# A batched two-layer MLP on one core: the framework's frame closed early, and results 4 to 7 on SyncE's ring

## The chip, the cores and the metric

The kernel runs on one core of one Trainium2 chip. The metric is the device time of one execution in microseconds (us). A profile of one execution comes with it; its span runs from the first to the last instruction of the program, and the execution's own time is a little longer than its span.

The core has five engines with a program each: PE (TensorE, matrix products), ACT (ScalarE), DVE (VectorE), POOL (GpSimd) and SP (SyncE, which here only waits and issues transfers). They meet through semaphores. Transfers go through 16 DMA engines that all queues share.

## What is computed

For each of 8 experts, 256 rows of `x` go through two matrices with a ReLU between them:

```python
n_experts, capacity, hidden, expert_hidden = 8, 256, 512, 2048
h = np.matmul(x, w1)          # x: [8, 256, 512]   w1: [8, 512, 2048]
h = np.maximum(h, 0)
return np.matmul(h, w2)       # w2: [8, 2048, 512]
```

All are float32 in memory: 4 MB of `x`, 32 MB of each weight, 4 MB of results.

## The kernel before

**Tiles and stages.** `w1` and `w2` of an expert are one transfer each (L96, L100; 4 MB read, 2 MB written, since the transfer casts to bfloat16). There are two buffers for each, so experts alternate; the last `w2` comes in two pieces (L103, L104). `x` comes in two halves of four experts: `x_f`, float32, issued by SP (L82), and `x_c`, cast by the transfer, issued by POOL (L106). ACT and DVE copy each half to `x_b`; PE transposes it (L203) to PSUM; DVE and ACT take it out to `xt` (L147, L145); DVE cuts an expert's part of it to `xe` (L151). For each expert PE then runs the first product (L215, 64 matmuls in four groups; ACT and DVE apply the ReLU to alternate groups, L167 and L185), then the second (L232, 32 matmuls), whose two halves DVE and ACT copy to the result buffer `o_sb` (L189, L169), which holds all 8 experts.

**Order.** Nothing is scheduled by a planner: the whole kernel is one critical section (L59) inside the frame that the Tile framework opens in `kernel` (L269), and each engine's order is written out. PE runs loops of its own, two turns for the transposes (L198) and four of two experts each (L206), and takes tokens from semaphores at L193. The loops over experts on the other engines are unrolled.

- SP issues `x_f` (L82), then waits in turn for each expert's weights and gives PE a token for each (L84 to L89). Then it waits for the last expert's result (L90, L91), issues it (L92, result 7), and at the end waits for all three transfers of results (L243).
- POOL issues `x_c`, then the weights of experts 0 and 1, with the identity matrix in between (L109, L111); each later load waits until PE has read the buffer (L123, L125). Behind the last load it issues results 0 to 5 as one transfer (L129) and, when expert 6 is done, result 6 (L132).

Transfers that one engine issues go through that engine's ring in order: POOL's is queue q0 in the profile, SP's is q1; q8 carries instructions.

**The frame.** Where the section begins, each engine branches into it (L269) on a semaphore that SP raises. Where it ends (L59), SP waits for every engine's drain; then the frame's end (L269) has each engine drain, meet the others, has POOL clear a range of semaphores, and has the engines meet once more. `no_gpsimd_drain=True` leaves POOL's drain out of the section's end, not out of the frame's.

Of the kernel before, what the change touches and what calls it, by code (L numbers as in the profile page):

```python
# [9 lines left out]
def kernel(  # L10
# [7 lines left out]
    nc = tc.nc  # L18
    P = 128
    bf = mybir.dt.bfloat16  # L20
    f32 = mybir.dt.float32
    relu = mybir.ActivationFunctionType.Relu

    E, C, H = x.shape
    F = w1.shape[2]
    MT = C // P
    KT1 = H // P
    KT2 = F // P
# [10 lines left out]
    def x_rows(g):  # L39
        return x[g * G:(g + 1) * G].rearrange("e c k -> (e c) k").rearrange(  # L40
            "(p j) k -> p j k", p=P
        )
# [13 lines left out]
    po = [nc.alloc_psum_tensor(f"pt_o{m}", [P, H], f32) for m in range(MT)]  # L56
    pt = [nc.alloc_psum_tensor(f"pt_tr{b}", [P, J, P], bf) for b in range(2)]

    with tc.tile_critical(no_gpsimd_drain=True):  # L59
        sem = nc.alloc_semaphore  # L60
        s_x = [sem(f"s_x{g}") for g in range(2)]
        s_w1 = [sem(f"s_w1_{e}") for e in range(E)]
        s_w2 = [sem(f"s_w2_{e}") for e in range(E)]
        s_w2b = sem("s_w2b")
        s_out = [sem(f"s_out{i}") for i in range(3)]
        s_id = sem("s_id")
        s_act = sem("s_act")
        s_dve = sem("s_dve")
        s_tr = sem("s_tr")
        s_h = sem("s_h")  # L70
        s_o = sem("s_o")
        t_xb = sem("t_xb")
        t_pt = [sem(f"t_pt{b}") for b in range(2)]
        t_xe = sem("t_xe")
        t_w = sem("t_w")
        t_ha = sem("t_ha")
        t_hb = sem("t_hb")

        sp, pool, act, dve, pe = nc.sync, nc.gpsimd, nc.scalar, nc.vector, nc.tensor


        sp.dma_start(x_f[:], x_rows(0)).then_inc(s_x[0], 16)  # L82
        for e in range(E):
            sp.wait_ge(s_w1[e], 16).then_inc(t_w, 1)  # L84
            if e < E - 1:
                sp.wait_ge(s_w2[e], 16).then_inc(t_w, 2)
            else:
                sp.wait_ge(s_w2[e], 16).then_inc(t_w, 1)
                sp.wait_ge(s_w2b, 16).then_inc(t_w, 1)  # L89
        sp.wait_ge(s_act, E)  # L90
        sp.wait_ge(s_dve, E)  # L91
        sp.dma_start(out_r[:, E - 1], o_sb[:, E - 1]).then_inc(s_out[2], 16)  # L92


        def load_w1(e):
            pool.dma_start(w1_sb[e % 2][:], w1_r[e]).then_inc(s_w1[e], 16)  # L96

        def load_w2(e):
            if e < E - 1:
                pool.dma_start(w2_sb[e % 2][:], w2_r[e]).then_inc(s_w2[e], 16)  # L100
            else:
                b = w2_sb[e % 2]
                pool.dma_start(b[:, :CUT], w2_r[e, :, :CUT]).then_inc(s_w2[e], 16)  # L103
                pool.dma_start(b[:, CUT:], w2_r[e, :, CUT:]).then_inc(s_w2b, 16)  # L104

        pool.dma_start(x_c[:], x_rows(1)).then_inc(s_x[1], 16)  # L106
        load_w1(0)
        load_w2(0)
        pool.memset(identity[:], 0.0).then_inc(s_id, 1)  # L109
        pool.wait_ge(s_id, 1)  # L110
        pool.affine_select(  # L111
            out=identity[:],
            in_=identity[:],
            compare_op=mybir.AluOpType.not_equal,
            fill=1.0,
            base=0,
            pattern=[[-1, P]],
            channel_multiplier=1,
        ).then_inc(s_id, 1)
        load_w1(1)  # L120
        load_w2(1)
        for e in range(2, E):
            pool.wait_ge(s_h, NQ * (e - 1))  # L123
            load_w1(e)
            pool.wait_ge(s_o, MT * (e - 1))  # L125
            load_w2(e)
        pool.wait_ge(s_act, E - 2)
        pool.wait_ge(s_dve, E - 2)
        pool.dma_start(out_r[:, :E - 2], o_sb[:, :E - 2]).then_inc(s_out[0], 16)  # L129
        pool.wait_ge(s_act, E - 1)  # L130
        pool.wait_ge(s_dve, E - 1)
        pool.dma_start(out_r[:, E - 2], o_sb[:, E - 2]).then_inc(s_out[1], 16)  # L132


        def take_x(g, half):

            for k in range(KT1):
                if k % 2 != half:
                    continue
                eng = act if half else dve  # L140
                eng.wait_ge(s_tr, g * KT1 + k + 1)
                src = pt[k % 2][:].rearrange("p (l m) q -> p l m q", m=MT)
                dst = xt[g][:, k].rearrange("p m (q l) -> p l m q", l=G)
                if half:
                    act.copy(dst, src).then_inc(t_pt[1], 1)  # L145
                else:
                    dve.tensor_copy(dst, src).then_inc(t_pt[0], 1)  # L147

        def give_xe(e):
            g, i0 = e // G, (e % G) * P  # L150
            dve.tensor_copy(xe[e % 2][:], xt[g][:, :, :, i0:i0 + P]).then_inc(t_xe, 1)  # L151


        HALF = J // 2
        act.wait_ge(s_x[0], 16)
        act.copy(x_b[:, :HALF], x_f[:, :HALF]).then_inc(t_xb, 1)  # L156
        take_x(0, 1)
        act.wait_ge(s_x[1], 16)
        act.wait_ge(s_tr, KT1)
        act.copy(x_b[:, :HALF], x_c[:, :HALF]).then_inc(t_xb, 1)  # L160
        take_x(1, 1)
        s_xt = sem("s_xt")
        act.drain().then_inc(s_xt, 1)  # L163
        for e in range(E):
            for q in range(0, NQ, 2):
                act.wait_ge(s_h, NQ * e + q + 1)
                act.activation(ht[e % 2][:, FB * q:FB * (q + 1), :], ph[0][:], relu).then_inc(t_ha, 1)  # L167
            act.wait_ge(s_o, MT * e + 2)
            act.copy(o_sb[:, e, 1, :], po[1][:]).then_inc(s_act, 1)  # L169


        dve.wait_ge(s_x[0], 16)
        dve.tensor_copy(x_b[:, HALF:], x_f[:, HALF:]).then_inc(t_xb, 1)  # L173
        take_x(0, 0)
        dve.wait_ge(s_x[1], 16)
        dve.wait_ge(s_tr, KT1)
        dve.tensor_copy(x_b[:, HALF:], x_c[:, HALF:]).then_inc(t_xb, 1)
        take_x(1, 0)
        dve.wait_ge(s_xt, 1)
        give_xe(0)  # L180
        give_xe(1)
        for e in range(E):
            for q in range(1, NQ, 2):
                dve.wait_ge(s_h, NQ * e + q + 1)
                dve.tensor_relu(ht[e % 2][:, FB * q:FB * (q + 1), :], ph[1][:]).then_inc(t_hb, 1)  # L185
            if e + 2 < E:
                give_xe(e + 2)
            dve.wait_ge(s_o, MT * e + 1)
            dve.tensor_copy(o_sb[:, e, 0, :], po[0][:]).then_inc(s_dve, 1)  # L189


        def take(s, n=1):
            pe.wait_ge(s, n).then_inc(s, -n)  # L193

        pe.wait_ge(s_id, 2)
        for b in range(2):
            pe.sem_inc(t_pt[b], 1)
        with pe.Fori(0, 2) as _g:  # L198
            take(t_xb, 2)
            for k in range(KT1):  # L200
                take(t_pt[k % 2])
                for j in range(J):
                    ins = pe.transpose(pt[k % 2][:, j], x_b[:, j, k::KT1], identity[:])  # L203
                ins.then_inc(s_tr, 1)

        with pe.Fori(0, E // 2) as _i:  # L206
            for b in range(2):
                take(t_xe)
                take(t_w)
                for q in range(NQ):  # L210
                    if q >= 2:
                        pe.wait_ge((t_ha, t_hb)[q % 2], 1)
                    for i in range(FB):
                        for kt in range(KT1):
                            ins = pe.matmul(  # L215
                                ph[q % 2][:, i, :],
                                w1_sb[b][:, kt, FB * q + i::KT2],
                                xe[b][:, kt],
                                start=(kt == 0),
                                stop=(kt == KT1 - 1),  # L220
                            )
                    ins.then_inc(s_h, 1)
                take(t_w)
                for kt in range(KT2):
                    if kt == 2 * FB:
                        take(t_ha, 2)
                    if kt == 3 * FB:
                        take(t_hb, 2)
                    if kt == CUT:
                        take(t_w)  # L230
                    for m in range(MT):
                        ins = pe.matmul(  # L232
                            po[m][:],
                            ht[b][:, kt, m * P:(m + 1) * P],
                            w2_sb[b][:, kt, :],
                            start=(kt == 0),
                            stop=(kt == KT2 - 1),
                        )
                        if kt == KT2 - 1:
                            ins.then_inc(s_o, 1)  # L240

        for s in s_out:
            sp.wait_ge(s, 16)  # L243


# [28 lines left out]
```

## Time and profile before

| | |
|---|---|
| median of 3 runs | 184.15 us (183.95 to 184.28) |
| the profiled execution | 184.07 us |
| its span | 182.3 us |
| PE busy in matmuls | 127.5 us, 70% |
| DVE, ACT, POOL busy | 39.4, 35.7, 11.8 us |
| granted TensorE clock, mean | 0.963 |
| read from and written to memory | 71.30 MB and 4.19 MB, 414 GB/s over the span |

Busy time of PE, DVE and ACT is work; an instruction that only waits, drains, branches or issues a transfer from SP isn't counted as busy. A DMA share is the busy share of the 16 DMA engines in a stretch. MB in the queues' rows are bytes as written, so a weight transfer counts 2 MB though 4 MB are read for it. A transfer's time to landing runs from its issue to the last of its 16 completion signals, one from each DMA engine. The rows of the profile stand where the prediction uses them.

### The profile page before, as it was taken

To read this page: it belongs to the slowest core of one execution; us is meant where nothing else is said; L and a number is where in the kernel's file an instruction comes from. 1 tells how busy PE (TensorE), PEld (TensorE's weight loads), DVE (VectorE), ACT (ScalarE), POOL (GpSimd) and SP (SyncE) were. 2 spreads that over 40 slices of the span, in tenths; PEclk is the share of its full clock that TensorE was granted. 3 is DMA by queue.
4 is the path that set the end of the run, shared out by engine and by line. 5 is a ranking of instruction groups with operands and counts; after the bars stand their busy time and mean duration, and the time that the engine had idled before them with its cause. 6 is when DMAs were issued, how large, how long until landed. Compare 5 with 4: busy or idle time off the path is not lost. (4 is left out here: it accounts for less than half of the span.)

```text
span 182.3 us, 1915 instructions
## 1 busy us (share of the span) xinstructions
PE 127.5 (70%) x832; PEld 90.0 (49%) x832; DVE 39.4 (22%) x38; ACT 35.7 (20%) x31; POOL 11.8 (6%) x26
## 2 busy tenths in 40 slices
PE   0006143999999794998677695949794989589910
PEld 0005142794794394339633682439642874198400
DVE  0025656023123123010501032012301040104010
ACT  2045856130230122002201220012201220122010
POOL 6100000001101101000101001010104000100000
PEclk9999999999999999699999999978999699999996
DMA  5999999999999999999999999999999999999990
GB/s 162 345 241 230 219 205 209 230 223 212 209 219 226 212 205 219 226 223 201 212 230 223 201 209 230 223 212 205 223 226 212 205 219 226 199 210 230 424 418 25
DMA packets 3810, 40.93 MB, mean 225 GB/s; under 512 B 352, under 2 KB 352, under 8 KB 1504
## 3 DMA queue, kind: packets, MB, share of 16 engines
q0 software_dynamic: 3520, 38.27, 94.2%
q1 hardware_dynamic: 288, 2.62, 4.0%
q8 instruction: 2, 0.03, 0.1%
HBM read 71.30 MB, written 4.19 MB: 414 GB/s over the span
## 5 line engine op out<-in xcount | busy, mean ns | idle before, releaser
L215 PE MATMUL pt_h<-xe,w_sb 128*128 128x256 bf16 x512 | 62.4, 286 | 15.8 <-PEq L193 15.8
L215 PEld LDWEIGHTS pt_h<-xe,w_sb 128*128 128x128 bf16 x512 | 58.6, 146 | 21.3 <-issue 18.9
L232 PE MATMUL pt_o<-w_sb,ht_sb 128*128 128x512 bf16 x256 | 58.2, 387 | 9.4 <-PEq L193 9.4
L232 PEld LDWEIGHTS pt_o<-w_sb,ht_sb 128*128 128x128 bf16 x256 | 25.2, 99 | 40.0 <-issue 12.6
L185 DVE TENSOR_SCALAR ht_sb<-pt_h 128x1024 bf16<-128x1024 f32 x16 | 19.6, 1224 | 61.7 <-PE pt_h L215 61.7
L167 ACT ACTIVATE ht_sb<-pt_h 128x1024 bf16<-128x1024 f32 x16 | 16.4, 1023 | 49.4 <-PE pt_h L215 49.4
L203 PE MATMUL pt_tr<-identity,x_b 128*128 128x128 bf16 x64 | 7.5, 308 | 21.4 <-PEq L193 21.4
L169 ACT COPY out_sb<-pt_o 128x512 f32<-128x512 f32 x8 | 4.7, 586 | 72.9 <-PE pt_o L232 72.9
L203 PEld LDWEIGHTS pt_tr<-identity,x_b 128*128 128x128 bf16 x64 | 6.4, 142 | 22.3 <-issue 22.1
L189 DVE COPY out_sb<-pt_o 128x512 f32<-128x512 f32 x8 | 5.5, 692 | 53.6 <-PE pt_o L232 53.6
L147 DVE COPY xt<-pt_tr 128x1024 bf16<-128x1024 bf16 x4 | 9.7, 2431 | 7.8 <-PE pt_tr L203 7.8
L145 ACT COPY xt<-pt_tr 128x1024 bf16<-128x1024 bf16 x4 | 9.7, 2434 | 6.8 <-PE pt_tr L203 6.8
L96 POOL DMA_DIRECT2D w_sb<-in_w_dram x8 | 4.3, 535 | 78.4 <-PE pt_h L215 78.2
L100 POOL DMA_DIRECT2D w_sb<-in_w_dram x7 | 3.7, 536 | 41.6 <-PE pt_o L232 41.6
L156 ACT CAST x_b<-x_f 128x2048 bf16<-128x2048 f32 x1 | 1.9, 1898 | 9.1 <-DMA x_f<-in_x_dram 9.1
L173 DVE CAST x_b<-x_f 128x2048 bf16<-128x2048 f32 x1 | 1.2, 1227 | 11.3 <-DMA x_f<-in_x_dram 11.3
L151 DVE COPY xe<-xt 128x1024 bf16<-128x1024 bf16 x8 | 3.3, 418 | 0.9 <-ACTq L163 0.9
L160 ACT COPY x_b<-x_c 128x2048 bf16<-128x2048 bf16 x1 | 2.0, 1957 | 0.0
L132 POOL DMA_DIRECT2D out_dram<-out_sb x1 | 0.5, 543 | 18.3 <-ACT out_sb L169 18.3
L156 ACT ACT_TABLE_LOAD x1 | 1.3, 1283 | 0.9 <-SPq L59 0.9
L103 POOL DMA_DIRECT2D w_sb<-in_w_dram x1 | 0.5, 528 | 7.5 <-PE pt_o L232 7.5
L129 POOL DMA_DIRECT2D out_dram<-out_sb x1 | 0.8, 846 | 0.0
(9 smaller groups left out, 2.8 us busy)
## 6 DMA issues: line engine op xcount, KB each, us to landing
w_sb<-in_w_dram POOLq DMA_DIRECT2D x15, 2048.0 KB, 30.3
out_dram<-out_sb POOLq DMA_DIRECT2D x1, 3072.0 KB, 37.7
x_f<-in_x_dram SPq DMA_DIRECT2D x1, 2048.0 KB, 10.3
w_sb<-in_w_dram POOLq DMA_DIRECT2D x1, 1152.0 KB, 27.0
x_c<-in_x_dram POOLq DMA_DIRECT2D x1, 1024.0 KB, 12.2
w_sb<-in_w_dram POOLq DMA_DIRECT2D x1, 896.0 KB, 30.8
out_dram<-out_sb POOLq DMA_DIRECT2D x1, 512.0 KB, 19.9
out_dram<-out_sb SPq DMA_DIRECT2D x1, 512.0 KB, 4.8
```

The source lines that it names most:

```text
L96: pool.dma_start(w1_sb[e % 2][:], w1_r[e]).then_inc(s_w1[e], 16)
L100: pool.dma_start(w2_sb[e % 2][:], w2_r[e]).then_inc(s_w2[e], 16)
L145: act.copy(dst, src).then_inc(t_pt[1], 1)
L147: dve.tensor_copy(dst, src).then_inc(t_pt[0], 1)
L151: dve.tensor_copy(xe[e % 2][:], xt[g][:, :, :, i0:i0 + P]).then_inc(t_xe, 1)
L167: act.activation(ht[e % 2][:, FB * q:FB * (q + 1), :], ph[0][:], relu).then_inc(t_ha, 1)
L169: act.copy(o_sb[:, e, 1, :], po[1][:]).then_inc(s_act, 1)
L185: dve.tensor_relu(ht[e % 2][:, FB * q:FB * (q + 1), :], ph[1][:]).then_inc(t_hb, 1)
L189: dve.tensor_copy(o_sb[:, e, 0, :], po[0][:]).then_inc(s_dve, 1)
L203: ins = pe.transpose(pt[k % 2][:, j], x_b[:, j, k::KT1], identity[:])
L215: ins = pe.matmul(ph[q % 2][:, i, :], w1_sb[b][:, kt, FB * q + i::KT2], xe[b][:, kt], start=(kt == 0), stop=(kt == KT1 - 1),)
L232: ins = pe.matmul(po[m][:], ht[b][:, kt, m * P:(m + 1) * P], w2_sb[b][:, kt, :], start=(kt == 0), stop=(kt == KT2 - 1),)
```

## The change

The section L59 now holds SP's first transfer alone. Behind it the frame is closed and compiled (`tc.close()`, `tc.compile()`), so the section's and the frame's end stand behind SP's issue of `x_f`. Everything else follows outside the frame, one level of indentation further out, on the same semaphores; two lists of them (`s_x`, `s_out`) are allocated ahead of the section and the rest behind it. At the end SP's wait for the three transfers of results is the program's last instruction.

Results go out in another split. POOL issues results 0 to 3 as one transfer and then drains; SP issues results 4 to 6 as one transfer once expert 6 is done, behind its loop over the weights' waits, and then result 7.

The streams of ACT, DVE and PE are the same as before but for their place. The diff without what is only indented anew:

```diff
+    sem = nc.alloc_semaphore
+    s_x = [sem(f"s_x{g}") for g in range(2)]
+    s_out = [sem(f"s_out{i}") for i in range(3)]
+
     with tc.tile_critical(no_gpsimd_drain=True):
-        sem = nc.alloc_semaphore
-        s_x = [sem(f"s_x{g}") for g in range(2)]
...
-        s_out = [sem(f"s_out{i}") for i in range(3)]
...
-        sp.dma_start(x_f[:], x_rows(0)).then_inc(s_x[0], 16)
+        nc.sync.dma_start(x_f[:], x_rows(0)).then_inc(s_x[0], 16)
+    tc.close()
+    tc.compile()
+
+    s_w1 = [sem(f"s_w1_{e}") for e in range(E)]
...
+    for e in range(E):
+        sp.wait_ge(s_w1[e], 16).then_inc(t_w, 1)
...
+    sp.wait_ge(s_act, E - 1)
+    sp.wait_ge(s_dve, E - 1)
+    sp.dma_start(out_r[:, G:E - 1], o_sb[:, G:E - 1]).then_inc(s_out[1], 16)
+    sp.wait_ge(s_act, E)
+    sp.wait_ge(s_dve, E)
+    sp.dma_start(out_r[:, E - 1], o_sb[:, E - 1]).then_inc(s_out[2], 16)
...
-        pool.wait_ge(s_act, E - 2)
-        pool.wait_ge(s_dve, E - 2)
-        pool.dma_start(out_r[:, :E - 2], o_sb[:, :E - 2]).then_inc(s_out[0], 16)
-        pool.wait_ge(s_act, E - 1)
-        pool.wait_ge(s_dve, E - 1)
-        pool.dma_start(out_r[:, E - 2], o_sb[:, E - 2]).then_inc(s_out[1], 16)
+    pool.wait_ge(s_act, G)
+    pool.wait_ge(s_dve, G)
+    pool.dma_start(out_r[:, :G], o_sb[:, :G]).then_inc(s_out[0], 16)
+    pool.drain()
...
+    for s in s_out:
+        sp.wait_ge(s, 16)
```

Here `E` is 8 and `G` is 4.

More of the change, by code (lines that the diff above doesn't have):

```diff
@@ L57 @@
     pt = [nc.alloc_psum_tensor(f"pt_tr{b}", [P, J, P], bf) for b in range(2)]
+    sem = nc.alloc_semaphore
+    s_x = [sem(f"s_x{g}") for g in range(2)]
+    s_out = [sem(f"s_out{i}") for i in range(3)]
     with tc.tile_critical(no_gpsimd_drain=True):
-        sem = nc.alloc_semaphore
-        s_x = [sem(f"s_x{g}") for g in range(2)]
-        s_w1 = [sem(f"s_w1_{e}") for e in range(E)]
-        s_w2 = [sem(f"s_w2_{e}") for e in range(E)]
-        s_w2b = sem("s_w2b")
-        s_out = [sem(f"s_out{i}") for i in range(3)]
@@ L66 @@
[L66 to L86, printed above, removed]
-            else:
[L88 to L126, printed above, removed]
@@ L127 @@
-        pool.wait_ge(s_act, E - 2)
-        pool.wait_ge(s_dve, E - 2)
-        pool.dma_start(out_r[:, :E - 2], o_sb[:, :E - 2]).then_inc(s_out[0], 16)
-        pool.wait_ge(s_act, E - 1)
-        pool.wait_ge(s_dve, E - 1)
-        pool.dma_start(out_r[:, E - 2], o_sb[:, E - 2]).then_inc(s_out[1], 16)
[L135 to L189, printed above, removed]
@@ L192, in take @@
-        def take(s, n=1):
-            pe.wait_ge(s, n).then_inc(s, -n)
-        pe.wait_ge(s_id, 2)
-        for b in range(2):
[L197 to L231, printed above, removed]
@@ new lines @@
+        nc.sync.dma_start(x_f[:], x_rows(0)).then_inc(s_x[0], 16)
+    tc.close()
+    tc.compile()
+    s_w1 = [sem(f"s_w1_{e}") for e in range(E)]
+    s_w2 = [sem(f"s_w2_{e}") for e in range(E)]
+    s_w2b = sem("s_w2b")
+    s_id = sem("s_id")
+    s_act = sem("s_act")
+    s_dve = sem("s_dve")
+    s_tr = sem("s_tr")
+    s_h = sem("s_h")
+    s_o = sem("s_o")
+    t_xb = sem("t_xb")
+    t_pt = [sem(f"t_pt{b}") for b in range(2)]
+    t_xe = sem("t_xe")
+    t_w = sem("t_w")
+    t_ha = sem("t_ha")
@@ new lines @@
+    t_hb = sem("t_hb")
+    sp, pool, act, dve, pe = nc.sync, nc.gpsimd, nc.scalar, nc.vector, nc.tensor
+    for e in range(E):
+        sp.wait_ge(s_w1[e], 16).then_inc(t_w, 1)
+        if e < E - 1:
+            sp.wait_ge(s_w2[e], 16).then_inc(t_w, 2)
+        else:
+            sp.wait_ge(s_w2[e], 16).then_inc(t_w, 1)
+            sp.wait_ge(s_w2b, 16).then_inc(t_w, 1)
+    sp.wait_ge(s_act, E - 1)
+    sp.wait_ge(s_dve, E - 1)
+    sp.dma_start(out_r[:, G:E - 1], o_sb[:, G:E - 1]).then_inc(s_out[1], 16)
@@ new lines, with load_w1, load_w2 @@
+    sp.wait_ge(s_act, E)
+    sp.wait_ge(s_dve, E)
+    sp.dma_start(out_r[:, E - 1], o_sb[:, E - 1]).then_inc(s_out[2], 16)
+    def load_w1(e):
+        pool.dma_start(w1_sb[e % 2][:], w1_r[e]).then_inc(s_w1[e], 16)
+    def load_w2(e):
+        if e < E - 1:
+            pool.dma_start(w2_sb[e % 2][:], w2_r[e]).then_inc(s_w2[e], 16)
+        else:
+            b = w2_sb[e % 2]
+            pool.dma_start(b[:, :CUT], w2_r[e, :, :CUT]).then_inc(s_w2[e], 16)
+            pool.dma_start(b[:, CUT:], w2_r[e, :, CUT:]).then_inc(s_w2b, 16)
@@ new lines @@
+    pool.dma_start(x_c[:], x_rows(1)).then_inc(s_x[1], 16)
+    load_w1(0)
+    load_w2(0)
+    pool.memset(identity[:], 0.0).then_inc(s_id, 1)
+    pool.wait_ge(s_id, 1)
+    pool.affine_select(
+        out=identity[:],
+        in_=identity[:],
+        compare_op=mybir.AluOpType.not_equal,
+        fill=1.0,
+        base=0,
+        pattern=[[-1, P]],
+        channel_multiplier=1,
+    ).then_inc(s_id, 1)
+    load_w1(1)
+    load_w2(1)
+    for e in range(2, E):
+        pool.wait_ge(s_h, NQ * (e - 1))
+        load_w1(e)
+        pool.wait_ge(s_o, MT * (e - 1))
+        load_w2(e)
@@ new lines, with take_x @@
+    pool.wait_ge(s_act, G)
+    pool.wait_ge(s_dve, G)
+    pool.dma_start(out_r[:, :G], o_sb[:, :G]).then_inc(s_out[0], 16)
+    pool.drain()
+    def take_x(g, half):
+        for k in range(KT1):
+            if k % 2 != half:
+                continue
+            eng = act if half else dve
+            eng.wait_ge(s_tr, g * KT1 + k + 1)
+            src = pt[k % 2][:].rearrange("p (l m) q -> p l m q", m=MT)
+            dst = xt[g][:, k].rearrange("p m (q l) -> p l m q", l=G)
+            if half:
+                act.copy(dst, src).then_inc(t_pt[1], 1)
+            else:
+                dve.tensor_copy(dst, src).then_inc(t_pt[0], 1)
@@ new lines, in give_xe @@
+    def give_xe(e):
+        g, i0 = e // G, (e % G) * P
+        dve.tensor_copy(xe[e % 2][:], xt[g][:, :, :, i0:i0 + P]).then_inc(t_xe, 1)
+    HALF = J // 2
+    act.wait_ge(s_x[0], 16)
+    act.copy(x_b[:, :HALF], x_f[:, :HALF]).then_inc(t_xb, 1)
+    take_x(0, 1)
+    act.wait_ge(s_x[1], 16)
+    act.wait_ge(s_tr, KT1)
+    act.copy(x_b[:, :HALF], x_c[:, :HALF]).then_inc(t_xb, 1)
+    take_x(1, 1)
+    s_xt = sem("s_xt")
+    act.drain().then_inc(s_xt, 1)
+    for e in range(E):
+        for q in range(0, NQ, 2):
+            act.wait_ge(s_h, NQ * e + q + 1)
+            act.activation(ht[e % 2][:, FB * q:FB * (q + 1), :], ph[0][:], relu).then_inc(t_ha, 1)
+        act.wait_ge(s_o, MT * e + 2)
+        act.copy(o_sb[:, e, 1, :], po[1][:]).then_inc(s_act, 1)
@@ new lines @@
+    dve.wait_ge(s_x[0], 16)
+    dve.tensor_copy(x_b[:, HALF:], x_f[:, HALF:]).then_inc(t_xb, 1)
+    take_x(0, 0)
+    dve.wait_ge(s_x[1], 16)
+    dve.wait_ge(s_tr, KT1)
+    dve.tensor_copy(x_b[:, HALF:], x_c[:, HALF:]).then_inc(t_xb, 1)
+    take_x(1, 0)
+    dve.wait_ge(s_xt, 1)
+    give_xe(0)
+    give_xe(1)
+    for e in range(E):
+        for q in range(1, NQ, 2):
+            dve.wait_ge(s_h, NQ * e + q + 1)
+            dve.tensor_relu(ht[e % 2][:, FB * q:FB * (q + 1), :], ph[1][:]).then_inc(t_hb, 1)
+        if e + 2 < E:
+            give_xe(e + 2)
+        dve.wait_ge(s_o, MT * e + 1)
+        dve.tensor_copy(o_sb[:, e, 0, :], po[0][:]).then_inc(s_dve, 1)
@@ new lines, in take @@
+    def take(s, n=1):
+        pe.wait_ge(s, n).then_inc(s, -n)
+    pe.wait_ge(s_id, 2)
+    for b in range(2):
+        pe.sem_inc(t_pt[b], 1)
+    with pe.Fori(0, 2) as _g:
+        take(t_xb, 2)
+        for k in range(KT1):
+            take(t_pt[k % 2])
+            for j in range(J):
+                ins = pe.transpose(pt[k % 2][:, j], x_b[:, j, k::KT1], identity[:])
+            ins.then_inc(s_tr, 1)
+    with pe.Fori(0, E // 2) as _i:
+        for b in range(2):
+            take(t_xe)
+            take(t_w)
+            for q in range(NQ):
+                if q >= 2:
+                    pe.wait_ge((t_ha, t_hb)[q % 2], 1)
+                for i in range(FB):
+                    for kt in range(KT1):
@@ L232 @@
                         ins = pe.matmul(
-                            po[m][:],
-                            ht[b][:, kt, m * P:(m + 1) * P],
-                            w2_sb[b][:, kt, :],
+                            ph[q % 2][:, i, :],
+                            w1_sb[b][:, kt, FB * q + i::KT2],
+                            xe[b][:, kt],
                             start=(kt == 0),
-                            stop=(kt == KT2 - 1),
+                            stop=(kt == KT1 - 1),
                         )
-                        if kt == KT2 - 1:
-                            ins.then_inc(s_o, 1)
@@ L242 @@
-        for s in s_out:
-            sp.wait_ge(s, 16)
+                ins.then_inc(s_h, 1)
+            take(t_w)
+            for kt in range(KT2):
+                if kt == 2 * FB:
+                    take(t_ha, 2)
+                if kt == 3 * FB:
+                    take(t_hb, 2)
+                if kt == CUT:
+                    take(t_w)
+                for m in range(MT):
+                    ins = pe.matmul(
+                        po[m][:],
+                        ht[b][:, kt, m * P:(m + 1) * P],
+                        w2_sb[b][:, kt, :],
+                        start=(kt == 0),
+                        stop=(kt == KT2 - 1),
+                    )
+                    if kt == KT2 - 1:
+                        ins.then_inc(s_o, 1)
```

## The prediction

> **What bounds the kernel now.** I read first the page's head and its DMA queues.
>
> ```profile
> span 182.3 us, 1915 instructions
> ...
> q0 software_dynamic: 3520, 38.27, 94.2%
> ```
>
> POOL's queue (q0) holds 94.2% of the 16 DMA engines' time. The same by stretches (columns: length, busy time of PE, PEld, DVE, ACT, POOL, granted clock, DMA share, GB/s):
>
> ```profile
> 0.00:1.90 1.90, 0.00 (x0) 0.00 (x0) 0.00 (x0) 0.99 (x1) 0.64 (x5) 1.00 0.00 0
> 1.90:5.80 3.90, 0.00 (x0) 0.00 (x0) 0.00 (x0) 0.29 (x1) 2.90 (x7) 1.00 1.02 328
> 5.80:168.00 162.20, 121.38 (x805) 87.43 (x806) 38.23 (x37) 33.81 (x29) 8.25 (x15) 0.97 1.02 219
> 168.00:178.00 10.00, 6.08 (x29) 2.55 (x26) 1.13 (x2) 0.58 (x1) 0.00 (x0) 1.00 1.01 413
> 178.00:179.60 1.60, 0.00 (x0) 0.00 (x0) 0.00 (x0) 0.00 (x0) 0.00 (x0) 0.86 0.06 26
> 179.60:182.30 2.70, 0.00 (x0) 0.00 (x0) 0.00 (x0) 0.00 (x0) 0.00 (x0) 0.50 0.03 6
> ```
>
> DMA share is 1.01 or 1.02 from 1.9 to 178 us (over 1 is rounding of the records). So only three stretches are open to a gain: 1.9 us ahead of the first byte, 1.6 us in which last packets and the completion come in, and 2.7 us behind, in which no engine computes and almost nothing is moved. The program's own chain of waits names PE and ACT at the end, because it follows instructions; PE has slack, as its waits show:
>
> ```profile
> PE pt_h L215 <- PEq L193: 15.8, 7, 3.2
> ```
>
> PE sits idle seven times, 15.8 us in all, ahead of a first stage; L193 is where it takes the weights' tokens.
>
> What lies in the last 2.7 us is seen under the source lines of the final wait (L243), the critical section's end (L59) and the Tile frame's end (L269); columns are duration in ns (min/median/max) and first and last start.
>
> ```profile
> L243 SPq EVENT_SEMAPHORE  x1: 28/28/28, 179.6 to 179.6; - x1
> ...
> L59 SPq EVENT_SEMAPHORE  x3: 17/28/28, 179.8 to 180.0; - x3
> ...
> L269 POOLq EVENT_SEMAPHORE  x4: 17/17/17, 181.7 to 182.2; - x4
> L269 POOLq DRAIN  x3: 45/78/1688, 179.9 to 182.0; - x3
> L269 SPq DRAIN  x3: 7/7/7, 180.2 to 181.9; - x3
> ```
>
> SP's wait for the results ends at 179.6. Then the section closes (0.6 us, to SP's first frame drain at 180.2), POOL's first drain takes 1.69 us from 179.9, and two rounds of semaphores take from 181.7 to 182.2.
>
> **The change part by part.** The profiled execution took 184.07 us: span 182.3 and 1.77 around it. The three runs' median is 184.15, 0.08 higher.
>
> *The end.* L59's and L269's tail no longer stands behind the last wait. The program ends with that wait: 182.3 - 179.6 = 2.7 us less. It could be less than that: POOL's 1.69 us drain might be owed in any case. The new drain on POOL's own stream stands behind its last DMA issue, which was at 139.3 in the profile before:
>
> ```profile
> L129 POOL DMA_DIRECT2D out_dram<-out_sb x1: 846/846/846, 139.3 to 139.3; - x1
> ```
>
> So even if it takes 1.69 us, or waits for the results it issued (they landed 37.7 us after issue, so 177.0), it ends ahead of 179.6. I take the whole 2.7; the bounds are 1.0 (2.7 - 1.69) and 2.7.
>
> *The start.* The same tail now runs behind SP's first issue, and POOL's, ACT's, DVE's and PE's streams wait for it. Before:
>
> ```profile
> 0.91 1.28 ACT L156 ACT_TABLE_LOAD   x1 [0.91 <-SPq L59]
> 0.95 0.38 SPq L82 DMA_DIRECT2D x_f<-in_x_dram  x1
> 1.46 0.67 POOL L106 DMA_DIRECT2D x_c<-in_x_dram  x1 [1.02 <-SPq L59]
> ```
>
> SP is done issuing at 0.95 + 0.38 = 1.33. The close takes 0.6 us to SP's frame drain and 0.55 us for the two rounds (181.7 to 182.2 and the last instruction), if POOL's drain is short; it has issued no transfer by then. The nearest drain of POOL without transfers behind it is in the program's entry, and its branch into the section shows when it got there:
>
> ```profile
> L269 POOLq COMPARE_BRANCH  x1: 33/33/33, 0.8 to 0.8; - x1
> ...
> L258 POOLq DRAIN  x1: 188/188/188, 0.3 to 0.3; - x1
> ```
>
> With 0.19 us the drain fits beside SP's part: the frame is closed at about 2.5. POOL's first issue came 0.66 us after the branch (1.46 - 0.8), so it now comes at 3.15, 1.7 us later than at 1.46. With a drain of 1.69 us it is 3.2 us later. Is that covered? The DMA queues by stretch:
>
> ```profile
> q1 hardware_dynamic: 3, 0.05, 10.6%
> ...
> q1 hardware_dynamic: 75, 1.23, 98.8%
> ...
> q0 software_dynamic: 15, 0.12, 83.6%
> ```
>
> The columns are packets, MB and the share of 16 engines. The first row is 0 to 2.0 us, the second 2.0 to 5.8: all DMA time goes to SP's `x_f`, though POOL has issued since 1.46. The last is 5.8 to 6.5: there POOL's data begin, some 4.4 us after its first issue. `x_f` is 128 packets of 16 KB (2.10 MB); 1.28 MB have started in these 78, so 50 are left at 5.8. These at the rate of a full engine (0.62 us for 16 KB, from 16 KB x 16 engines at 0.42 MB/us, nearly the 413 GB/s above) are 50 / 16 x 0.62 = 1.95 us: alone, `x_f` would occupy the engines until 7.75. POOL's data, 1.7 us later, begin at 7.5. Nothing is idle; the cover is 1.9 us deep and 0.2 is left. I take 0; with the long drain the engines idle 3.2 - 1.9 = 1.3 us. The other end is a gain of nothing, since the first byte's time is set by SP's issue, which doesn't move.
>
> The Trainium skill, "DMA: Bandwidth & Descriptors", section "Latency and other measured facts", puts the first byte of a GpSimd transfer at about 1 us. The row above shows 4.4 here, behind a busy queue; by the page the long drain would cost nothing, since data could begin at 4.7 + 1.0 = 5.7, and rival 2 below would come out at 181.45 instead of 182.75.
>
> ```profile
> 11.26 1.23 DVE L173 CAST x_b<-x_f 128x2048 bf16<-128x2048 f32 x1 [11.26 <-DMA x_f<-in_x_dram]
> ...
> w_sb<-in_w_dram POOLq DMA_DIRECT2D x15, 2048.0 KB, 30.3
> ```
>
> `x_f` itself, undisturbed, lands near 8.3 (7.75 and some 0.5 for the completion) instead of 11.26, and casts and transposes move up nearly 3 us. That goes nowhere: PE reaches expert 0 earlier and then waits for weights whose stream begins with the same bytes and ends at the same time. POOL's loads take 30.3 us from issue to landing, against 9.6 us in which the queue moves one (2.10 MB at 219 GB/s), so issuing them 3 us earlier or 2 us later adds no hole. ACT's table load (1.28 us at 0.91) moves to about 2.5 and still ends before `x_f` lands.
>
> *Results 4 to 6 on SP's ring.* Bytes are the same. SP can issue them only when the loop of weight waits is through:
>
> ```profile
> L89 SPq EVENT_SEMAPHORE  x1: 17/17/17, 169.6 to 169.6; - x1
> ...
> 174.73 0.35 SPq L92 DMA_DIRECT2D out_dram<-out_sb  x1
> ...
> q0 software_dynamic: 261, 1.01, 102.2%
> ```
>
> The last row is POOL's queue in 174.0 to 176.4: SP's result 7, issued at 174.73, got no packet until 176.4, so its first bytes took up to 1.7 us. Three results cost at most 3 x 0.35 = 1.05 us to issue: bytes from 169.65 + 1.05 + 1.7 = 172.4 at the latest. POOL's ring now has 2.1 MB from 168 on, at 413 GB/s until 173.1, so the engines stay fed and 4.19 MB end at 178 as before. Result 7 stands behind 4 to 6 on its ring instead of beside POOL's; it is the last to finish either way. SP is free again by 170.8, well ahead of 174.6 when it must issue result 7. Cost 0; if the cover of 0.7 us is missed, up to 1 us.
>
> *Instruction packets.* One 16 KB packet of PE's program lies in the stream:
>
> ```profile
> q8 instruction: 2, 0.03, 0.1%
> ...
> q8 instruction: 1, 0.02, 2.9%
> ```
>
> The first row is the whole span, the second 43 to 45 us: 2.9% of 16 engines over 2 us is 0.93 us, all on one engine, which is then late to the end (178.0 to 179.6 is its tail, with a share of 0.06, about one engine of 16). The second packet isn't in that stretch; in 179.6 to 182.3 the DMA share of 0.03 has nothing else to be, so it came behind the last wait. I keep one in the stream; none would give back up to 0.9, two would take 0.9.
>
> Sum: 184.07 - 2.7 + 0 + 0 + 0 = 181.37, and 0.08 to the median: **181.45**. Its own range: 180.55 (no packet in the stream) to 182.5 (a little idle at the start or the seam).
>
> **The rivals.**
>
> 1. The frame's end waits for `x_f`. The section holds a transfer, and if its close waits until that lands (8.3), POOL issues first at 8.3 + 1.15 + 0.66 = 10.1, its data begin at 14.5, and the engines idle from 7.75: 6.75 us. 181.45 + 6.75 = 188.2, slower. It decides once POOL's first issue is later than 1.46 + 1.9 + 2.7 = 6.1. For it: a frame is closed only when its work is over. Against: SP's drains took 7 ns, and the semaphore that `x_f` counts up is the kernel's own.
> 2. POOL's drain takes 1.69 us at the start too: 181.45 + 1.3 = 182.75. Against it is the 188 ns row.
> 3. A second instruction packet falls into the stream, since PE's code is laid out anew: 181.45 + 0.9 = 182.35. For it: the second packet came just when PE left its last wait, and PE now leaves its program earlier, while results are moved. The Trainium skill, "Runtime: NRT & Kernel Launch", section "Instruction fetch mechanics", says that a taken branch to a page outside the window forces a fetch. By that, each turn of PE's loops would fetch; here the trace shows two packets in all.
> 4. The tail isn't saved but paid outside: POOL's drain, or a like one, remains behind the last wait. Then 1.0 us is gained: 183.15, and no change if the rounds remain too.
>
> **How the numbers follow.** Chances: forecast 0.52; rival 1 0.15; rival 2 0.12; rival 3 0.13; rival 4 0.08, half of it no change. 0.2% of 184.15 is 0.37 us, so faster is below 183.78 and slower above 184.52. Faster: 0.52 + 0.12 + 0.13 + 0.04 = 0.81; same 0.04; slower 0.15. The range from 180.5 to 183.2 holds the forecast, rivals 2 and 3 and the first half of 4, some 8 in 10; rival 1 lies outside. The likeliest's own range is 180.55 to 182.5.
>
> **What would show it.** Right: the last instruction of the span is SP's wait for the three results near 179.6, with no drain or round behind it; POOL's first issue near 3.1 and q0's first share near 7.5; a DMA share of 1 without a hole from 1.9 to 178; `x_f` landing near 8.3; q1 beside q0 from about 171; time less span still near 1.8. Wrong: a hole in the DMA row between 7 and 15 us (rival 1 or 2, told apart by POOL's first issue: 10 or 4.7), two q8 packets before 178 (rival 3), a hole near 173, or a time less span above 2.5 (rival 4).

## The result and the profile after

| | before | after |
|---|---|---|
| median | 184.12 us (183.95 to 184.28, 4 runs) | 180.77 us (180.60 to 180.90, 4 runs) |
| the profiled execution | 184.07 | 180.70 |
| its span | 182.3 | 179.4 |
| time less span | 1.77 | 1.30 |

The ratio is 0.9817, with a 95% interval from 0.98 to 0.9834: 3.35 us faster. Of the profiled executions' 3.37 us, 2.9 lie in the span and 0.47 outside it. Of the changed kernel's four runs three had 1.30 to 1.34 of time less span; the fourth, the slowest at 180.90, had 2.20, with a span of 178.7. The runs don't show what that one waited for.

First the DMA row before, then the head of the changed kernel's page with its DMA row and queues:

```profile
DMA  5999999999999999999999999999999999999990
...
span 179.4 us, 1898 instructions
...
DMA  5999999999999999999999999999999999999996
...
q0 software_dynamic: 3120, 36.70, 93.5%
q1 hardware_dynamic: 688, 4.19, 6.2%
q8 instruction: 1, 0.02, 0.0%
```

The DMA row has no hole, and its last slice, a 0 before, is now a 6: the kernel ends soon after the last transfers. The stretches say it in numbers (columns as before: length, busy time of PE, PEld, DVE, ACT, POOL, clock, DMA share, GB/s):

```profile
0.00:1.90 1.90, 0.00 (x0) 0.00 (x0) 0.00 (x0) 0.00 (x0) 0.20 (x4) 1.00 0.00 0
1.90:6.70 4.80, 0.00 (x0) 0.00 (x0) 0.00 (x0) 1.28 (x1) 3.33 (x7) 1.00 1.02 348
6.70:168.00 161.30, 120.94 (x792) 87.80 (x800) 37.46 (x36) 33.83 (x29) 7.62 (x14) 0.96 1.02 218
168.00:178.00 10.00, 7.21 (x35) 3.22 (x34) 1.92 (x2) 0.59 (x1) 0.00 (x0) 1.00 1.00 410
178.00:179.40 1.40, 0.00 (x0) 0.00 (x0) 0.00 (x0) 0.00 (x0) 0.00 (x0) 1.00 0.07 26
```

The transfers still run from 1.9 to 178 with a share of 1. The stretch of 2.7 us behind the last wait is gone. Its instructions are now near the start, as the source lines show: L249 is the last wait, L67 the closed frame, L138 the drain that the change put at the end of POOL's stream.

```profile
L249 SPq EVENT_SEMAPHORE  x2: 17/22/28, 178.1 to 179.4; - x2
...
L67 POOLq EVENT_SEMAPHORE  x4: 17/17/17, 1.7 to 2.2; - x4
L67 POOLq DRAIN  x3: 34/41/65, 0.7 to 2.1; - x3
...
L138 POOLq DRAIN  x1: 37065/37065/37065, 139.1 to 139.1; - x1
```

POOL's three drains of the frame take 0.03 to 0.07 us there, where the first took 1.69 before. The drain at L138 takes 37.07 us: it begins right behind the issue of results 0 to 3 and ends at 176.1, after they have landed (139.1 and 36.2 to landing, so 175.3).

The start of the changed kernel, from the timeline (start, duration, what):

```profile
0.95 0.38 SPq L65 DMA_DIRECT2D x_f<-in_x_dram  x1
2.34 1.28 ACT L162 ACT_TABLE_LOAD   x1 [2.34 <-PEq L67]
2.85 0.67 POOL L114 DMA_DIRECT2D x_c<-in_x_dram  x1 [2.40 <-POOLq L67]
...
10.45 1.90 ACT L162 CAST x_b<-x_f 128x2048 bf16<-128x2048 f32 x1 [6.83 <-DMA x_f<-in_x_dram]
```

SP issues when it did; POOL issues 1.4 us later than before (2.85 against 1.46). The DMA queues of this kernel from 2.0 to 6.7 us (first row) and from 6.7 to 7.4 (the others), in packets, MB and share:

```profile
q1 hardware_dynamic: 99, 1.62, 100.9%
...
q0 software_dynamic: 9, 0.07, 50.5%
q1 hardware_dynamic: 9, 0.15, 49.8%
```

POOL's data begin at 6.7, some 3.9 us behind its first issue and only 0.9 us later than before. From there the two queues share the engines, so `x_f` lands at about 10.45, where its casts begin, and not much earlier than the 11.26 of before.

The end: SP's two issues of results in the timeline, then the queues from 169.5 to 172.6 (q0) and from 172.6 to 178.1 (q1).

```profile
169.56 0.39 SPq L97 DMA_DIRECT2D out_dram<-out_sb  x1
...
175.91 0.34 SPq L100 DMA_DIRECT2D out_dram<-out_sb  x1
...
q0 software_dynamic: 320, 1.31, 102.6%
...
q1 hardware_dynamic: 532, 2.07, 91.9%
```

Results 4 to 6, issued by SP at 169.56, get nothing until POOL's ring is nearly through at 172.6; then SP's ring follows without a hole. PE ran its last first stage more slowly here (8.56 us instead of 7.18; its mean granted clock from 160 to 163 us was 0.55, where it was 1.00 before), so result 7 was issued at 175.91 instead of 174.73. The kernel ended no later for it: in the repeat below, result 7 was issued at 174.39, landed 5.2 us after its issue instead of 3.4, and the span was 179.6. The queue of transfers sets the end.

### The profile page after: what moved, and what is told of

Read it like the earlier page. It is cut to its first block, busy times and chain, and to the rows that moved or that the text cites. A ratio compares the mean times of both kernels' runs of the same rounds, so it can differ in the third digit from the quotient of the medians.

```text
span 179.4 us, 1898 instructions
## 1 busy us (share of the span) xinstructions
PE 128.1 (71%) x824; PEld 91.0 (51%) x832; DVE 39.4 (22%) x38; ACT 35.7 (20%) x31; POOL 11.2 (6%) x25
## 5 line engine op out<-in xcount | busy, mean ns | idle before, releaser
L221 PE MATMUL pt_h<-xe,w_sb 128*128 128x256 bf16 x512 | 64.3, 292 | 15.8 <-PEq L199 15.8
L221 PEld LDWEIGHTS pt_h<-xe,w_sb 128*128 128x128 bf16 x512 | 59.6, 147 | 22.1 <-issue 18.8
L238 PE MATMUL pt_o<-w_sb,ht_sb 128*128 128x512 bf16 x248 | 56.5, 387 | 10.7 <-PEq L199 10.6
L173 ACT ACTIVATE ht_sb<-pt_h 128x1024 bf16<-128x1024 f32 x16 | 16.4, 1024 | 51.2 <-PE pt_h L221 51.2
L114 POOL DMA_DIRECT2D x_c<-in_x_dram x1 | 0.7, 672 | 2.4 <-POOLq L67 2.4
L137 POOL DMA_DIRECT2D out_dram<-out_sb x1 | 0.8, 766 | 0.0
## 6 DMA issues: line engine op xcount, KB each, us to landing
out_dram<-out_sb POOLq DMA_DIRECT2D x1, 2048.0 KB, 36.2
```

The lines of the kernel that those rows point to most:

```text
L221: ins = pe.matmul(ph[q % 2][:, i, :], w1_sb[b][:, kt, FB * q + i::KT2], xe[b][:, kt], start=(kt == 0), stop=(kt == KT1 - 1),)
L238: ins = pe.matmul(po[m][:], ht[b][:, kt, m * P:(m + 1) * P], w2_sb[b][:, kt, :], start=(kt == 0), stop=(kt == KT2 - 1),)
```

## The experiments

Each was timed beside runs of the kernel before on the same chip; the ratios are to these, the brackets 95% intervals. A repeat of the changed kernel serves as reference. Differences to it are between medians, and the chips aren't all the same: the kernel before had medians of 183.82 to 184.12 on them, so differences of 0.2 or 0.3 us across chips show nothing.

**The changed kernel again.**

> The changed kernel unaltered, on the same chip as the three that follow, as what they are compared with: 180.5 to 180.9, time less span 1.3.

180.74 us, 0.9822 [0.9808, 0.9835]. Time less span was 1.27 to 1.35 in its five runs.

**The new split in the old frame.** POOL sends 0 to 3, SP sends 4 to 6 and 7, the frame ends where it did:

```diff
+        sp.wait_ge(s_act, E - 1)
+        sp.wait_ge(s_dve, E - 1)
+        sp.dma_start(out_r[:, G:E - 1], o_sb[:, G:E - 1]).then_inc(s_out[1], 16)
...
-        pool.dma_start(out_r[:, :E - 2], o_sb[:, :E - 2]).then_inc(s_out[0], 16)
...
+        pool.dma_start(out_r[:, :G], o_sb[:, :G]).then_inc(s_out[0], 16)
```

> The kernel before with the new split of the results alone: POOL sends 0 to 3, SP sends 4 to 6 and 7; the frame ends behind the last wait. Theory: POOL's drain in the frame's end costs its 1.69 us whenever it comes first after transfers, however long ago they landed, so time stays 184.1 (within 0.2). Rival (the drain's time depends on how long ago POOL's last transfer landed, 178.4 before, 175.3 with the split): the drain shortens and the time falls to 182.5 to 183.5.

183.97 us, 1.0001 [0.9991, 1.0011]: no change. POOL's drain in the frame's end:

```profile
L269 POOLq DRAIN  x3: 40/78/1615, 179.7 to 181.7; - x3
```

It still takes 1.62 us although POOL's last transfer landed some 3 us earlier than before (175.3 against 178.4). So the first drain behind transfers kept its price when they had ended 4 us ago instead of 1.5.

**The old split in the new frame.** The same edit the other way round, with POOL's drain kept at the end of its stream:

```diff
-    pool.wait_ge(s_act, G)
-    pool.wait_ge(s_dve, G)
-    pool.dma_start(out_r[:, :G], o_sb[:, :G]).then_inc(s_out[0], 16)
+    pool.wait_ge(s_act, E - 2)
+    pool.wait_ge(s_dve, E - 2)
+    pool.dma_start(out_r[:, :E - 2], o_sb[:, :E - 2]).then_inc(s_out[0], 16)
+    pool.wait_ge(s_act, E - 1)
+    pool.wait_ge(s_dve, E - 1)
+    pool.dma_start(out_r[:, E - 2], o_sb[:, E - 2]).then_inc(s_out[1], 16)
     pool.drain()
```

> The changed frame, but the results split as before: POOL sends 0 to 5 and 6, SP sends 7; POOL's drain still stands last on its stream. Theory (the drain waits for the landing of what POOL issued and then takes some 1.66 us: in the changed kernel it began at 139.1, took 37.07 us and so ended at 177.0, 1.66 us behind the landing at 175.3): result 6 on POOL's ring lands near 178.1, the drain ends near 179.8, behind SP's last wait at 179.4, so span 179.8 and time 181.1 to 181.3. Rival (the split is worth nothing, as predicted): 180.8, last instruction is SP's wait.

180.90 us, 0.9829 [0.9816, 0.9842]; the changed kernel's 0.9822 lies inside the interval. The expectation's sum was off: in the changed kernel the drain ended at 176.1 and not at 177.0, so 0.8 us behind the landing and not 1.66. Here it is

```profile
L138 POOLq DRAIN  x1: 21017/21017/21017, 158.3 to 158.3; - x1
```

and ends at 179.3, still ahead of SP's last wait at 179.7. So the split isn't what makes the kernel faster; the old one only brings POOL's drain to within 0.4 us of the end. Time less span was 1.40 to 1.72 in these runs against 1.27 to 1.35.

**No drain at all.**

```diff
-    pool.drain()
```

> The changed kernel without the drain at the end of POOL's stream. Theory: the drain lies wholly beside other work, so 180.8, same span 179.4. Rival 1 (something outside the program then waits for POOL's transfers in its place): time less span grows from 1.3 to about 3 and the time to 182.4. Rival 2 (the drain took something from POOL or the queues): below 180.6.

180.69 us, 0.9817 [0.9798, 0.9837]; time less span 1.27 to 1.35. The drain costs nothing where it stands, and nothing waits in its place when it is gone.

**The drain last.**

```diff
-    pool.drain()
...
     for s in s_out:
         sp.wait_ge(s, 16)
+    for s in s_out:
+        pool.wait_ge(s, 16)
+    pool.drain()
```

> The changed kernel, but POOL waits for all three transfers of results ahead of its drain, so the drain stands behind the last landing. Theory: it takes its fixed 1.66 to 1.69 us there, span 181.0 to 181.1 and time 182.4. Rival (a drain with nothing outstanding for a while is short, 0.04 to 0.19 us as at the start): 180.9 to 181.0.

183.14 us, 0.995 [0.9937, 0.9962]: 2.4 us above the changed kernel, more than the expected 182.4.

```profile
L251 POOLq DRAIN  x1: 1600/1600/1600, 179.5 to 179.5; - x1
```

The drain gives 1.6 us, and the span is 181.1 as expected; but time less span is 1.81 to 2.13, about 0.6 more than the changed kernel's. No expectation had that; the next two runs ask where it comes from.

**Which engine ends last.** In the first, POOL waits for the three transfers at its end, behind its drain; in the second, ACT, DVE and PE do and POOL doesn't. These waits end with SP's, so the span doesn't move.

```diff
     for s in s_out:
         sp.wait_ge(s, 16)
+    for s in s_out:
+        pool.wait_ge(s, 16)
```

> The changed kernel, but behind its drain POOL waits for all three transfers of results, so POOL's program ends with SP's. Theory (what follows a program's end takes about 1.9 us on POOL and 1.3 on SP, since time less span is 1.3 where SP ends last and 1.9 to 2.1 where POOL does): span as before it, time less span 1.9, time 181.3. Rival (time less span hangs on the drain, or on the frame's end): 1.3 and 180.7.

181.39 us, 0.9854 [0.9839, 0.987]. The span stayed at 179.1 to 179.7 and time less span went to 1.86 to 2.13, with one run at 2.9.

```diff
     for s in s_out:
         sp.wait_ge(s, 16)
+    for eng in (act, dve, pe):
+        for s in s_out:
+            eng.wait_ge(s, 16)
```

> The changed kernel, but ACT, DVE and PE wait for all three transfers of results at the end of their programs, POOL not. Theory that POOL alone has the longer end: time less span stays 1.3, time 180.7. Rival (any engine that ends last beside SP adds the 0.5 us): 181.2 or more.

181.17 us, 0.9842 [0.9827, 0.9856], time less span 1.57 to 1.75. So it isn't POOL alone: POOL's late end adds 0.6 us outside the span, a late end of the other three 0.35. In the kernel before, all five ended together behind the last round of semaphores, and its 46 runs beside these experiments had 1.72 to 2.03. That 0.5 us is what the change gains outside the span. What is done there after a program's end the trace doesn't show.

**POOL's start put off.** POOL first fills a piece of the result buffer, which is overwritten later (1024 columns, then 3072):

```diff
+    pool.memset(o_sb[:, E - 1:], 0.0)
+    pool.drain()
     pool.dma_start(x_c[:], x_rows(1)).then_inc(s_x[1], 16)
```

> The changed kernel with POOL's first issue put off by one fill of 128x1024 float32 and a drain (some 1 us). In the changed kernel POOL issued first at 2.85, its data began at 6.75, and of the 128 packets of x_f 102 had started by 6.7, so 26 were left: 26 / 16 x 0.62 = 1.0 us of cover. Theory (only what exceeds the cover costs time): 180.8 to 181.1. Rival (every delay of POOL's start costs time one to one): 181.8.

> The same with a fill three times as large (some 3 us). Theory: the engines idle for the delay less 1.0 us of cover, near 2 us: 182.7 to 183.0, with a hole in the DMA row ahead of 12 us and the last weights landing 2 us later. Rival 1 (one to one): 183.8. Rival 2 (the DMA has slack later on that takes it up): 180.8.

180.76 us, 0.9839 [0.982, 0.9857], and 181.54 us, 0.989 [0.9868, 0.9913]. The shorter delay costs nothing that the intervals separate; the longer one 0.8 us in the medians (180.74 to 181.54) and in the spans' medians (179.4 to 180.2), 1.2 by the ratios, where near 2 us were expected. In the first of them POOL's issue in the timeline, then the queues from 5.6 to 7.6 (q1) and from 7.6 to 8.0 (q0):

```profile
3.92 0.68 POOL L116 DMA_DIRECT2D x_c<-in_x_dram  x1 [0.63 <-issue]
...
q1 hardware_dynamic: 52, 0.85, 99.7%
...
q0 software_dynamic: 8, 0.07, 79.8%
```

The same of the second:

```profile
5.62 0.68 POOL L116 DMA_DIRECT2D x_c<-in_x_dram  x1 [0.63 <-issue]
...
q1 hardware_dynamic: 54, 0.87, 101.3%
...
q0 software_dynamic: 8, 0.07, 91.7%
...
L94 SPq EVENT_SEMAPHORE  x1: 17/17/17, 170.0 to 170.0; - x1
```

In both, POOL's data begin at about 7.6, when 2.00 of `x_f`'s 2.10 MB have started, though one issued at 3.92 and the other at 5.62. So from issue to data it takes at most 2.0 us. The time from issue to data falls as POOL issues later: 4.4 before, 3.9 in the changed kernel, 3.7 and 2.0 here. That fits time spent behind SP's packets, and not a fixed lead time. With the longer delay the last weights land 0.6 us later than in the changed kernel (170.0 against 169.4). Most of that is lost near the start: POOL's data moved from 0 to 13 us are, in the changed kernel and with the longer delay,

```profile
q0 software_dynamic: 150, 1.23, 45.1%
...
q0 software_dynamic: 139, 1.13, 43.9%
```

while `x_f` is through in both. The 0.10 MB take about 0.5 us at 219 GB/s. A hole isn't seen in the shares, so that the cover is used up at 5.62 is the likely reading and not shown.

**The frame closed ahead of SP's first transfer.**

```diff
     with tc.tile_critical(no_gpsimd_drain=True):
-        nc.sync.dma_start(x_f[:], x_rows(0)).then_inc(s_x[0], 16)
+        nc.sync.nop()
     tc.close()
     tc.compile()
+    nc.sync.dma_start(x_f[:], x_rows(0)).then_inc(s_x[0], 16)
```

> The changed kernel with x_f issued by SP as its first instruction behind the closed frame instead of ahead of its close; the section holds an empty instruction of SP. Theory: the first byte moves with SP's issue, from 0.95 to about 2.2 (1.3 us later), and with it the whole stream of transfers: 182.0 to 182.1. Rival (the start isn't what counts, x_f is covered anyway): 180.8.

181.59 us, 0.9888 [0.9863, 0.9912]: 0.85 us above the changed kernel by the medians, 1.2 by the ratios.

```profile
1.87 0.38 SPq L68 DMA_DIRECT2D x_f<-in_x_dram  x1
```

SP issues 0.92 us later and not 1.3, since the close is quicker with no issue inside; the stream of transfers and the end move with it. So it counts that SP's transfer stands ahead of the close, and POOL's may stand behind it.

**PE's loop written out.**

```diff
-    with pe.Fori(0, E // 2) as _i:
+    for _i in range(E // 2):
```

> The changed kernel with PE's loop over pairs of experts written out: some 1600 instructions of PE instead of 470 and about five more 16 KB packets of program in the stream of transfers. Theory (each packet costs one DMA engine 0.93 us, and that engine sets the end): span longer by about 4.5 us, time 185, with the last signal of each transfer further behind the others from expert to expert. Rival (the packets are taken up, or fall on several engines): below 181.5.

180.74 us, 0.9832 [0.9818, 0.9845]: no change. The page has

```profile
q8 instruction: 6, 0.10, 0.2%
```

six packets of instructions instead of one, and span 179.4. The theory falls: more packets of this kind don't add up to a later end. The completion signals of its transfers in the trace suggest why. Ahead of the first packet one of a weight transfer's 16 signals comes more than 0.75 us behind the first of them; behind each packet there is one more, and 7 behind the sixth. The last signal of the last weights is no later for it: 1.42 us behind the first, against 1.44 in the changed kernel. So the packets seem to have fallen on an engine each. What the first packet costs was not tried.

**No frame at all.** The section, `tc.close()` and `tc.compile()` are left out, and the kernel is called without the framework:

```diff
-    with tc.tile_critical(no_gpsimd_drain=True):
-        nc.sync.dma_start(x_f[:], x_rows(0)).then_inc(s_x[0], 16)
-    tc.close()
-    tc.compile()
+    nc.sync.dma_start(x_f[:], x_rows(0)).then_inc(s_x[0], 16)
```

> The changed kernel with no Tile frame at all: SP's first transfer and all that follows stand on the kernel's own semaphores from the start. Theory (the closed frame costs only what it puts ahead of SP's issue, the two instructions between 0.73 and 0.95; e7's issue 0.92 us later cost 0.85): SP issues near 0.75, time 180.5 to 180.6, 0.2 less than the changed kernel. Rival (the close still costs through POOL's late start): 180.0 or less, by 1 us or more.

180.60 us, 0.9817 [0.9803, 0.983].

```profile
0.74 0.38 SPq L64 DMA_DIRECT2D x_f<-in_x_dram  x1
1.25 0.67 POOL L111 DMA_DIRECT2D x_c<-in_x_dram  x1 [0.81 <-POOLq L261]
```

SP issues 0.21 us earlier; the median is 0.14 lower than the changed kernel's, which the intervals don't separate. POOL issues 1.6 us earlier and that brings nothing more. So the closed frame costs about 0.2 us at most.

## Why the prediction was right, and where it was not

**The end, right.** The 2.7 us behind the last wait were saved whole, as forecast; putting the drain alone back there brings 1.6 of them back into the span. The wait itself ended at 179.4 instead of 179.6, a difference smaller than that of spans from run to run (178.7 to 179.6).

**The 1.77 us around the span, missed.** This is the term of the sum that was mis-sized: it was taken to stay 1.77 and became 1.30. With 0.2 us of the span it makes up the 0.7 by which 181.45 was too high. The two runs on who ends last show that it depends on the other four engines being through before SP. Rival 4 looked in the right place, but with the wrong sign.

**The start, right in its cost, wrong in its reason.** POOL's drain was short (0.04, not the 0.19 used), and POOL issued 1.4 us later, not 1.7. The cost of 0 held, but not for the reason given. The step that read 4.4 us between POOL's first issue and its data as a lead time, and so left 0.2 us of cover, failed: the lead time is at most 2.0 us, and the rest of the 4.4 was, as it seems, waiting behind `x_f`. POOL may issue at 3.92 for nothing and at 5.62 for 0.8 us. By the same error `x_f` was expected to land near 8.3 and landed at 10.45: POOL's data came in from 6.7 and shared the engines. The sentence of the Trainium skill, "DMA: Bandwidth & Descriptors", section "Latency and other measured facts", about 1 us to the first byte, was nearer than the 4.4; measured here is at most 2.0 us from the issue, which itself takes 0.68. It follows that rival 2, at 1.3 us, was priced too high: POOL's issue would have come at 4.7, between the two delays tried (3.92 and 5.62), and so would have cost no more than the longer one, 0.8 by the medians.

**The results on SP's ring, right.** Cost 0 in both directions, in the old frame and in the new one. The bound of 172.4 for SP's first bytes was missed by 0.2 us, because SP's packets waited until POOL's ring was nearly dry; no hole came of it, for the same reason. The 1.7 us in that bound had been read with the same error as the 4.4, as a lead time while the other ring was busy.

**The rivals.** Rival 1 didn't come: the frame closed at 2.3 us while `x_f` was still on its way until 10.4. Rival 3 didn't come in the result's profile, which has one packet, but it did in the repeat's: from 172.5 to 174.5 us, while results were moved, that has

```profile
q8 instruction: 1, 0.02, 3.0%
```

beside the one near 42 us. This run took 180.95 us, the longest of its five, but only 0.2 above their median. So the price of 0.9 us was too high, and five further packets in the unrolled kernel cost nothing.

## What to carry to other kernels

Where transfers bind from the first byte to the last, only what stands ahead of the first and behind the last is worth time, so a frame's closing work belongs behind the first issue, where the transfer covers it, not behind the last wait. A time from issue to data that is read while another queue is busy is a bound on the lead time, not the lead time; ask what that queue was doing before spending the difference as cover. Time less span isn't a constant of the setup: let all engines but one be through before the last wait.

## What the runs showed of the hardware that was not expected

A drain on POOL waits for the transfers that POOL has issued (37.07 us in the changed kernel), and the first one behind transfers costs 1.6 to 1.7 us even when all have landed (1.69, 1.62 and 1.60); with no transfer of POOL's ahead of them, the frame's three took 0.03 to 0.07. What lies outside the span is about 1.3 us where SP alone ends last (1.27 to 1.48 in 39 of 41 runs; the other two had 2.20 and 2.46), 1.57 to 1.75 with ACT, DVE and PE, and 1.81 to 2.13 with POOL, but for one run at 2.9. Between two busy rings the turn didn't come at once: SP's ring got no packet for 3 us (169.56 to 172.6) while POOL's had work, although earlier, from 6.7 us on, the two shared the engines about evenly.
